# One token-gate phase ahead of the blocks: S5 and gate columns in seven block products over 1024 tokens, gates kept in DRAM

## The chip, the cores and the metric

The kernel runs on one core of one Trainium2 chip. The metric is the device time in microseconds (us) of one execution; of several runs the median counts. Engines are called PE (TensorE), DVE (VectorE), ACT (ScalarE), POOL (GpSimd) and SP (SyncE, which here only issues DMAs).

## The reference

The kernel is one gated layer over x (2048 tokens, 1024 columns, float32). Cut to what matters here:

```python
hn = rmsnorm(x, norm_w)
proj = hn @ w_in                     # 1024 x 10264 columns, split into the pieces below
ha = mlstm_chunkwise(aq, ak, av, i_pre, logf)       # branch a, recurrent in chunks
hb = gla_chunkwise(bq, bk, bv, log_a)               # branch b, recurrent in chunks
yc = gelu(s5_ssm(cu, ...))                          # branch c, 32 groups, scan over all 2048 tokens
yc = yc * sigmoid(yc @ s5_w_glu) * silu(cz)
ga, gb, gc = split(sigmoid(g), 3)                   # g: 3 x 1024 columns of proj
merged = ga * (ya @ w_a) + gb * (yb @ w_b) + gc * (yc @ w_c)
out = rmsnorm(x + merged @ w_out, final_norm)
```

The columns cu (512), cz (512) and g (3072) of proj need nothing but hn. The S5 scan needs cu of all tokens.

## The kernel before, in words

Every large product keeps float32 precision by splitting both operands into a rounded part "hi" and a rest "lo", and adding three matmuls: hi·hi, hi·lo, lo·hi. For a weight tile ACT makes hi by a copy (L85) and DVE makes lo by a subtraction (L86, function `split`); in some places POOL subtracts (L99, L105). A full product of 512 tokens by 512 columns over 1024 inputs is `dense_fm` (L110): 8 slices k, 4 column tiles, 3 terms, so 96 matmuls of 128x512 (L122 to L124).

Tokens go in four blocks b of 512. **Ahead of the blocks** stands a pre-phase over b = 3, 2, 1, 0: `norm(b)` (rmsnorm, transposes by PE at L192, split), `proj_c` (the columns u = cu and z = cz, each one `dense_fm`; the split u weights are kept for all four blocks), `spill(b)` (split hn of a block to DRAM, L197), and two pieces q of `s5_mats` (L930 on: the S5 matrices of four groups, eight pieces in all, made by DVE and POOL together at L948 to L977). `s5_setup` (L765 on) computes small S5 tables in some 200 DVE instructions.

**A block** then goes through `gla_in`, two `gla_pair`, `mlstm_gates` (its transposes at L513 mark a fixed place of each block), two `mlstm_pair`, and for the branches bi = 1, 0, 2: `gate(bi, f)` for two halves f (96 matmuls each, tanh by ACT at L654 into tiles `sg`), `branch` (`yl` tiles read back from DRAM at L664 to L669; matmuls with w_bb, w_ba, w_bc; DVE multiplies by the gate at L674, POOL adds at L679). `c_final` finishes S5's output for the block with a glu product, `start(b+1)` brings hn of the next block from DRAM and begins it, `tail` does w_out and the last norm. In block 0 the S5 scan itself, `s5_main` for 16 q's of two groups (L1005 to L1053), is put between the branches: matmuls zp (L1034), a copy by ACT, a swap of partition halves by two DMAs that ACT issues (L1025, L1026), a product by POOL (L1027), two DVE instructions (L1028, L1029), a DVE scan, a second such rotation, and matmuls yp (L1047, L1048).

A scheduler orders the instructions on each engine ahead of time; on the chip each engine runs its list in order, and SP and ACT issue their DMAs in order too.

Of the kernel before, what the change touches and what calls it, by code (L numbers as in the profile page):

```python
# [12 lines left out]
ALU = mybir.AluOpType  # L13
# [43 lines left out]
def hybrid_kernel(ctx: ExitStack, tc: tile.TileContext, a):  # L57
# [24 lines left out]
    z_d = dram.tile([NB, 4, 128, TB], F32, name="z_d")  # L82

# [6 lines left out]
    def wload(src, k, n, keep=None):  # L90
        if keep is not None and k in keep:
            return keep[k]
        raw = w_p.tile([128, 512], F32, tag="raw", name="raw", bufs=RB)
        nc.sync.dma_start(out=raw[:, 0:n], in_=src(k))
        if keep is not None:
            t = keep["pool"].tile([128, 2, 512], F32R, tag="keep", name="keep", bufs=KD)
            keep[k] = t[:, 0, :], t[:, 1, :]
            nc.scalar.copy(out=t[:, 0, :], in_=raw)
            nc.gpsimd.tensor_tensor(out=t[:, 1, :], in0=raw, in1=t[:, 0, :].bitcast(F32), op=ALU.subtract)  # L99
            return keep[k]  # L100
# [9 lines left out]
    def dense_fm(src, nk, n, tiles, rhs, evict, keep=None, cuts=1):  # L110
# [4 lines left out]
        for i in range(cuts):  # L115
            ts = slice(i * TB // cuts, (i + 1) * TB // cuts)
            for k in range(nk):
                hi, lo = wload(src, k, n, keep)
                rh, rl = rhs(k)
                for m, (o, mm) in enumerate(tiles):  # L120
                    pm = ps[m][0:mm, ts]
                    nc.tensor.matmul(pm, lhsT=hi[:, o:o + mm], rhs=rh[:, ts], start=(k == 0), stop=False)  # L122
                    nc.tensor.matmul(pm, lhsT=hi[:, o:o + mm], rhs=rl[:, ts], start=False, stop=False)  # L123
                    nc.tensor.matmul(pm, lhsT=lo[:, o:o + mm], rhs=rh[:, ts], start=False, stop=(k == nk - 1))  # L124
# [24 lines left out]

    def rsqrt(dst, src, n, pool, scale):  # L150
        v = pool.tile([128, 8], F32, tag="rsq", name="rsq", bufs=4)
        nc.vector.tensor_scalar(out=v[:, 0:n], in0=src, scalar1=scale, scalar2=EPS, op0=ALU.mult, op1=ALU.add)
        nc.gpsimd.tensor_tensor(out=dst, in0=v[:, 0:n], in1=mhalf[:, 0:n], op=ALU.pow)

    mat_d = dram.tile([32 // GB, 128, 3, GB, 128], F32, name="mat_d")
    cs_d = dram.tile([32 // GB, 128, GB, 2, NJ], F32, name="cs_d")
    rho = const.tile([128, 32], F32, name="rho")
    s5_cm = tc.tile_pool(name="s5", bufs=1, side="right")
    s5 = s5_cm.__enter__()
    hn = {}  # L160

    def hn_rhs(k):
        return hn[k // 4][:, k % 4, 0, :], hn[k // 4][:, k % 4, 1, :]

    with tc.tile_pool(name="pre", bufs=2) as pre:
        nwb = pre.tile([128, DM], F32, name="nwb", bufs=1)
        hns = {}
        keep = {"pool": pre}

        def norm(b):  # L170
            hb = []
            for g in range(2):
                t = (pre if b % 2 else hn_p).tile([128, 4, 2, TB], F32R, tag="hn", name="hn", bufs=2)
                hb.append(t)
            hns[b] = hb
            for c in range(NC):
                r0 = b * TB + c * CH
                xt = pre.tile([128, DM], F32, tag="xt", name="xt")
                nc.sync.dma_start(out=xt, in_=x[r0:r0 + CH, :])
                if b == NB - 1 and c == 0:  # L180
                    nc.sync.dma_start(out=nwb, in_=a["norm_w"].partition_broadcast(128))
                xn = pre.tile([128, DM], F32, tag="xn", name="xn")
                ss = pre.tile([128, 1], F32, tag="ss", name="ss")
                nc.scalar.activation(out=xn, in_=xt, func=AF.Square, accum_out=ss)
                rs = pre.tile([128, 1], F32, tag="rs", name="rs")
                rsqrt(rs, ss, 1, pre, 1.0 / DM)
                nc.vector.scalar_tensor_tensor(out=xn, in0=xt, scalar=rs, in1=nwb, op0=ALU.mult, op1=ALU.mult)
                for g in range(2):
                    pt = psm.tile([128, 4, 128], F32, tag="m", name="pt")
                    for i in range(4):  # L190
                        k = g * 4 + i
                        nc.tensor.transpose(pt[:, i, :], xn[:, k * 128:(k + 1) * 128], ident)  # L192
                    split(hb[g][:, :, 0, c * CH:(c + 1) * CH], hb[g][:, :, 1, c * CH:(c + 1) * CH], pt)

        def spill(b):
            for g in range(2):
                nc.sync.dma_start(out=hnd[b, :, 4 * g:4 * g + 4], in_=hns[b][g].bitcast(F32))  # L197

        def proj_c(b, part):
            hb = hns[b]  # L200

            def rhs(k):
                return hb[k // 4][:, k % 4, 0, :], hb[k // 4][:, k % 4, 1, :]

            def ev_u(m, ps):
                us = pre.tile([128, T8, JB], F32, tag="us", name="us")
                nc.scalar.copy(out=us, in_=ps.rearrange("p (j s) -> p s j", s=T8))
                nc.sync.dma_start(
                    out=u_d[:, 8 * m:8 * m + 8, :, b * JB:(b + 1) * JB].rearrange("s g h j -> (g h) s j"), in_=us)

            def ev_z(m, ps):
                th = pre.tile([128, TB], F32, tag="th", name="th")
                nc.scalar.activation(out=th, in_=ps, func=AF.Tanh, scale=0.5)
                zt = pre.tile([128, TB], F32, tag="zt", name="zt")
                nc.vector.scalar_tensor_tensor(out=zt, in0=th, scalar=1.0, in1=ps, op0=ALU.add, op1=ALU.mult)  # L215
                nc.sync.dma_start(out=z_d[b, m], in_=zt)

            if part == 0:
# [8 lines left out]
        for b in range(NB - 1, -1, -1):  # L227
            if b < NB - 1:
                proj_c(b, 0)
# [943 lines left out]
```

## Time and profile before

| quantity | value |
|---|---|
| median of 3 runs | 2986.44 us (2984.15 to 2987.95) |
| the profiled execution, its own time | 2983.99 us |
| its span in the trace | 2982.2 us |
| mean granted PE clock, share of full speed | 0.986 |
| busy: PE, PEld (weight load) | 96%, 82% |
| busy: DVE, ACT, POOL | 58%, 42%, 31% |
| DMA, mean over the span | 127 GB/s |

The span is what the trace covers; the execution's own time is 1.8 us longer. Matmuls are pipelined: each record lasts some 0.39 us while the next starts 0.23 us later, so the busy share of PE says little, and the count of matmuls in a stretch more. "PEclk" is the clock that was granted to PE, 1.00 being full speed.

### The profile page before, as it was taken

What the parts mean: (1) busy time and instruction counts of PE and PEld (TensorE: products, weight loads), DVE (VectorE), ACT (ScalarE), POOL (GpSimd) and SP (SyncE); (2) the same over time, 40 slices, a digit from 0 to 9 for tenths busy, and PEclk for the clock granted to TensorE, in tenths of its full rate; (3) what the DMA queues carried; (4) which work ended last, traced back from release to release, by engine and by line L of the source; (5) the groups of instructions that cost most, each with busy time, mean ns of one, the idle gap of its engine ahead of it and who ended that gap; (6) DMA issues with size and microseconds to landing.
All of it is one profiled execution on the core that took longest, in us unless ns stands there. A gap on an engine that the chain in (4) does not pass through costs nothing. (4 is left out here: it accounts for less than half of the span.)

```text
span 2982.2 us, 41294 instructions
## 1 busy us (share of the span) xinstructions
PE 2857.7 (96%) x14360; PEld 2446.0 (82%) x14360; DVE 1738.8 (58%) x3289; ACT 1257.8 (42%) x2512; POOL 912.1 (31%) x783
## 2 busy tenths in 40 slices
PE   7898899999889999999999999999999999999998
PEld 7677889887668798988888798988888798897886
DVE  8766675645465666665434558555434658656335
ACT  4324444432224544444333644444334544444333
POOL 3453453212330345231122245231122345321122
PEclk9999999999999999999999999999999999999999
DMA  7665223336866332334434332334445332334433
GB/s 246 227 207 168 63 75 103 103 104 165 227 194 215 106 109 75 92 85 118 143 117 157 121 103 64 98 89 122 137 117 169 112 95 69 98 94 145 144 114 103
DMA packets 291442, 379.74 MB, mean 127 GB/s; under 512 B 83936, under 2 KB 194960, under 8 KB 288928
## 3 DMA queue, kind: packets, MB, share of 16 engines
q1 hardware_dynamic: 286112, 368.70, 41.7%
q10 hardware_dynamic: 5120, 8.39, 1.1%
q8 instruction: 113, 1.85, 0.3%
q14 instruction: 97, 0.79, 0.1%
HBM read 302.33 MB, written 65.04 MB: 123 GB/s over the span
## 5 line engine op out<-in xcount | busy, mean ns | idle before, releaser
L86 DVE TENSOR_TENSOR wlo<-raw,whi 128x512 fp32r<-128x512 f32 (+2 forms) x736 | 551.8, 754 | 774.7 <-ACT whi L85 625.1
L85 ACT CAST whi<-raw 128x512 fp32r<-128x512 f32 (+2 forms) x736 | 421.0, 576 | 714.1 <-PE d L123 440.3
L122 PE MATMUL d<-hn,whi 128*128 128x512 f32 x1472 | 588.2, 400 | 13.8 <-ACT whi L85 12.5
L123 PE MATMUL d<-hn,whi 128*128 128x512 f32 x1472 | 581.2, 395 | 0.0
L124 PE MATMUL d<-hn,wlo 128*128 128x512 f32 x1472 | 552.4, 397 | 5.3 <-DVE wlo L86 4.9
L139 PE MATMUL d<-wlo,hn 128*128 128x384 f32 (+1 forms) x1280 | 440.7, 344 | 12.1 <-DVE wlo L86 9.9
L140 PE MATMUL d<-whi,hn 128*128 128x384 f32 (+1 forms) x1280 | 433.8, 339 | 0.0
L105 POOL TENSOR_TENSOR wlo<-raw,whi 128x384 fp32r<-128x384 f32 x208 | 237.3, 1141 | 529.4 <-ACT whi L104 348.4
L138 PE MATMUL d<-whi,hn 128*128 128x384 f32 (+1 forms) x1280 | 387.0, 347 | 2.6 <-DVE zt L215 1.6
L122 PEld LDWEIGHTS d<-hn,whi 128*128 128x128 f32 x1472 | 278.8, 189 | 78.0 <-ACT whi L85 16.0
L124 PEld LDWEIGHTS d<-hn,wlo 128*128 128x128 f32 x1472 | 277.5, 189 | 68.3 <-DVE wlo L86 7.7
L123 PEld LDWEIGHTS d<-hn,whi 128*128 128x128 f32 x1472 | 278.4, 189 | 57.2 <-issue 0.9
L139 PEld LDWEIGHTS d<-wlo,hn 128*128 128x128 f32 x1280 | 242.0, 189 | 19.3 <-DVE wlo L86 12.8
L138 PEld LDWEIGHTS d<-whi,hn 128*128 128x128 f32 x1280 | 236.0, 189 | 11.4 <-issue 2.9
L140 PEld LDWEIGHTS d<-whi,hn 128*128 128x128 f32 x1280 | 242.1, 189 | 0.5 <-issue 0.2
L669 POOL TENSOR_TENSOR yl<-yraw,yl 128x512 fp32r<-128x512 f32 x64 | 83.9, 1310 | 447.2 <-ACT yl L668 400.9
L122 PE MATMUL d<-yl,whi 128*128 128x512 f32 x512 | 204.6, 401 | 4.0 <-ACT whi L85 1.7
L123 PE MATMUL d<-yl,whi 128*128 128x512 f32 x512 | 202.6, 396 | 0.0
L104 ACT CAST whi<-raw 128x384 fp32r<-128x384 f32 x208 | 106.2, 510 | 201.8 <-PE d L140 141.2
L124 PE MATMUL d<-yl,wlo 128*128 128x512 f32 x512 | 188.6, 397 | 2.4 <-DVE wlo L86 2.4
L679 POOL TENSOR_TENSOR sg<-sg 128x512 f32<-128x512 f32 x64 | 92.8, 1477 | 108.4 <-DVE sg L674 108.4
L539 DVE SCALAR_TENSOR_TENSOR cacc<-craw,convw,cacc 128x512 f32<-128x512 f32 x144 | 121.7, 845 | 2.7
(334 smaller groups left out, 4647.9 us busy)
## 6 DMA issues: line engine op xcount, KB each, us to landing
raw<-in_w_in_dram SPq DMA_DIRECT2D x480, 192.0 KB
raw<-in_w_in_dram SPq DMA_DIRECT2D x232, 256.0 KB
yraw<-y_a SPq DMA_DIRECT2D x64, 256.0 KB
raw<-in_w_out_dram SPq DMA_DIRECT2D x64, 256.0 KB
hnd<-hn SPq DMA_DIRECT2D x6, 2048.0 KB
y_a<-ys SPq DMA_DIRECT2D x64, 192.0 KB
raw<-in_w_bb_dram SPq DMA_DIRECT2D x48, 256.0 KB
raw<-in_w_ba_dram SPq DMA_DIRECT2D x48, 256.0 KB
```

Of the source, the lines that this page charges most:

```text
L85: nc.scalar.copy(out=hi, in_=src)
L86: nc.vector.tensor_tensor(out=lo, in0=src, in1=hi.bitcast(F32), op=ALU.subtract)
L104: nc.scalar.copy(out=hi[:, 0:n], in_=raw[:, 0:n])
L105: nc.gpsimd.tensor_tensor(out=lo[:, 0:n], in0=raw[:, 0:n], in1=hi[:, 0:n].bitcast(F32), op=ALU.subtract)
L122: nc.tensor.matmul(pm, lhsT=hi[:, o:o + mm], rhs=rh[:, ts], start=(k == 0), stop=False)
L123: nc.tensor.matmul(pm, lhsT=hi[:, o:o + mm], rhs=rl[:, ts], start=False, stop=False)
L124: nc.tensor.matmul(pm, lhsT=lo[:, o:o + mm], rhs=rh[:, ts], start=False, stop=(k == nk - 1))
L138: nc.tensor.matmul(ps[c][:, 0:n], lhsT=lh[:, cs], rhs=hi[:, 0:n], start=(k == 0), stop=False)
L139: nc.tensor.matmul(ps[c][:, 0:n], lhsT=lh[:, cs], rhs=lo[:, 0:n], start=False, stop=False)
L140: nc.tensor.matmul(ps[c][:, 0:n], lhsT=ll[:, cs], rhs=hi[:, 0:n], start=False, stop=(k == nk - 1))
L539: nc.vector.scalar_tensor_tensor(out=acc, in0=raw[:, i:TB + i], scalar=convw[:, t, i:i + 1], in1=acc, op0=ALU.mult, op1=ALU.add)
L679: nc.gpsimd.tensor_tensor(out=acc[i], in0=acc[i], in1=sg[m], op=ALU.add)
```

## The change

A new function `early` takes the place of the pre-phase, and all work on the columns u, z and g moves there, for two blocks of tokens (a "pair": blocks 2 and 3 first, then 0 and 1) at a time.

One **quad** treats 256 columns by 1024 tokens over 1024 inputs. Weights and tokens are each cut into 2 by 2 halves; seven products of half size, with sums and differences of halves as operands, replace eight. A product is 4 slices by 3 terms, 12 matmuls of 128x512, so a quad has 84 matmuls. The token side (tiles T0 to T6, split into hi and lo) is built once per pair; the weight side per quad: POOL forms four sums or differences, ACT copies seven hi parts, DVE (5) and POOL (2) subtract for lo, and four evictions go through DVE, ACT and SP. Pair 1 has 14 quads (z0, z1, g0 to g11; u of these blocks is done by an ordinary product, `plain_u`), pair 0 has 16 (u, z, g).

In pair 1, after each of the quads j = 2 to 9, stands one piece of `s5_mats` and `ahead`, the norm of a quarter of block 0 or 1, put to DRAM. `second_load` and `second_pair` then build T0 to T6 of pair 0. In pair 0 the steps of `s5_main` are spread over quads 3 to 15. The tanh of the gates is stored in DRAM (`g_d`, 96 tiles of 256 KB) and `gate` in a block only loads it. In a block `c_final` now stands right behind `mlstm_pair`, the branches follow with no gate matmuls between them, and `start(b+1)` and `tail` close every block.

The core of the diff (after's lines; `...` marks what is left out):

```diff
-    def gate(bi, f):
+    def gate(b, bi, f):
         sg = []
-        def ev(m, ps):
+        for m in range(4):
             t = tl.tile([128, TB], F32, tag="t2", name="sg", bufs=T2B)
-            nc.scalar.activation(out=t, in_=ps, func=AF.Tanh, scale=0.5)
+            nc.sync.dma_start(out=t, in_=g_d[b, 8 * bi + 4 * f + m])
             sg.append(t)
-        dense_fm(win(GT + bi * DM + f * 512, 512), KD, 512, full(512), hn_rhs, ev)
         return sg
...
         acc = {}
-        for i, bi in enumerate((1, 0, 2)):
-            sg = [gate(bi, f) for f in range(2)]
...
+        c_final(nc, a, mx, tl, b, dskip, u_d, y_d, z_d, y_a, dense_fm, split, full)
+        for bi in (1, 0, 2):
+            sg = [gate(b, bi, f) for f in range(2)]
             yl = {}
             for f in range(2):
                 branch(b, acc, bi, f, sg[f], yl)
-                if b == 0 and i < 2:
-                    s5_steps(...)
-        if b and b + 1 < NB:
+        if b + 1 < NB:
             gi = start(b + 1)
         tail(b, acc)
...
+def early(tc, nc, a, hn_p, ident, rho, rsqrt, D):
+        def quad(c0, done):
+            raw = big("raw")...
+            nc.sync.dma_start(out=raw, in_=a["w_in"]...[:, :, c0:c0 + 256])
...
+            G.tensor_tensor(out=s1, in0=a21, in1=a22, op=A_)
+            G.tensor_tensor(out=s2, in0=s1, in1=a11, op=SB)
+            G.tensor_tensor(out=a21, in0=a11, in1=a21, op=SB)
...
+            product(pa, split(a11, V), 0, True, False)
+            ACT.copy(out=p1, in_=pa)
+            product(pb, split(s2, G), 1, True, False)
+            V.tensor_tensor(out=u2, in0=pb, in1=p1, op=A_)
+            G.tensor_tensor(out=s2, in0=a12, in1=s2, op=SB)
+            product(pa, split(a12, V), 2, False, True)
+            done(0, 0, pa, None)
+            product(pb, split(a21, V), 3, False, False)
+            V.tensor_tensor(out=u3, in0=pb, in1=p1, op=A_)
+            product(pc, split(s1, G), 4, True, False)
+            done(1, 1, pc, u3)
+            product(pb, split(a22, V), 5, False, True)
+            done(1, 0, pb, p1)
+            product(pc, split(s2, V), 6, False, True)
+            done(0, 1, pc, u2)
...
+        order = [("z", 0), ("z", 1)] + [("g", i) for i in range(12)]
...
+            for j, y in enumerate(order[:10]):
+                run(*y, 1)
+                if j >= 2:
+                    s5_mats(..., j - 2)
+                    ahead((j - 2) // 4, (j - 2) % 4)
...
+            F = second_load(hp)
+            for y in order[10:]:
+                run(*y, 1)
+            second_pair(F)
...
+            for j, y in enumerate([("u", 0), ("u", 1)] + order):
+                run(*y, 0)
+                to = max(0, min(n5, n5 * (j - 1) // 13))
+                for i in range(at, to):
+                    ... next(s5q[i - LAG[s]]) ...
```

In the whole program the matmuls of 128x512 for these columns go from 3072 (2304 for the gates, 768 for u and z) to 2712 (30 quads of 84, 192 for `plain_u`).

How the rows stand on three engines. **POOL in the stage of the S5 matrices.** In before one piece of `s5_mats` reads (m, P, W, fm are its tiles, `mk` a cleared one):

```order
L957 TENSOR_TENSOR m_1604<-raw_1598,pw 128x576
L959 TENSOR_TENSOR P_1613<-m_1604,m_1605 128x576
L957 TENSOR_TENSOR m_1604<-w_1606,pw 128x4x128
L959 TENSOR_TENSOR W_1617<-m_1604,m_1605 128x512
L975 TENSOR_TENSOR fm_1622<-low,high 128x512
L999 MEMSET mk 128x512
L975 TENSOR_TENSOR fm_1622<-low,high 128x512
L975 TENSOR_TENSOR fm_1632<-low,high 128x512 x2
```

In after the same piece (L1142 to L1184 now) stands between the quads' sums (s, raw; L857 to L859, L871) and lo parts (hl, L839):

```order
L857 TENSOR_TENSOR s_2210<-raw 128x512
L859 TENSOR_TENSOR raw<-raw 128x4x128
L1142 TENSOR_TENSOR m_2109<-raw_2103,pw 128x576
L858 TENSOR_TENSOR s_2211<-s_2210,raw 128x512
L1184 MEMSET mk 128x512
L1144 TENSOR_TENSOR P_2118<-m_2109,m_2110 128x576
L1142 TENSOR_TENSOR m_2109<-w_2111,pw 128x4x128
L1144 TENSOR_TENSOR W_2122<-m_2109,m_2110 128x512
L1160 TENSOR_TENSOR fm_2127<-low,high 128x512
L89 TENSOR_TENSOR rs<-rsq,mhalf 128x1
L1160 TENSOR_TENSOR fm_2127<-low,high 128x512
L839 TENSOR_TENSOR hl<-s_2211,hl 128x512
```

Two more fm, one hl and one s (L871) follow before the next quad: 14 large instructions per quad on POOL where the piece alone had eight.

**SP at the start.** In after the split hn of blocks 2 and 3 (hn, t_100 and T_91, 2 MB each) is written to DRAM ahead of loads of x (xt) and of the first quad's weights (raw, 1 MB):

```order
L738 DMA uraw<-in_w_in_dram 128x512 x3
L731 DMA hnd<-hn 128x4096 x2
L699 DMA xt<-in_x_dram 128x1024 x3
L754 DMA u_d<-us 128x8x64 x2
L738 DMA uraw<-in_w_in_dram 128x512
L699 DMA xt<-in_x_dram 128x1024
L754 DMA u_d<-us 128x8x64 x2
L738 DMA uraw<-in_w_in_dram 128x512 x7
L731 DMA hnd<-t_100 128x4096
L731 DMA hnd<-T_91 128x4096
L852 DMA raw<-in_w_in_dram 128x8x256
```

In before the same queue loads x and the first weights with no store between them; the loads of the first two token quarters and weights read:

```order
L179 DMA xt<-in_x_dram 128x1024
L181 DMA nwb<-in_norm_w_dram 128x1024
L179 DMA xt<-in_x_dram 128x1024
L94 DMA raw<-in_w_in_dram 128x512 x5
```

**ACT in the S5 scan.** In before the issues of the swaps stand almost alone among a few casts of weights (whi):

```order
L1035 COPY uz_6892<-zp 128x512
L1025 DMA ra_6899<-uz_6892 64x512
L1026 DMA ra_6899<-uz_6892 64x512
L1035 COPY uz_6918<-zp 128x512
L1025 DMA ra_6925<-uz_6918 64x512
L1026 DMA ra_6925<-uz_6918 64x512
L85 CAST whi<-raw 128x512 x2
L1025 DMA ra_6899<-ra_6899 64x512
```

In after one q is in the swaps at a time, and the quads' casts (hl) and tanh (sg) stand behind each issue:

```order
L1220 COPY uz_4926<-zp 128x512
L1210 DMA ra_4942<-uz_4926 64x512
L1211 DMA ra_4942<-uz_4926 64x512
L908 ACTIVATE sg<-pa 128x512
L838 CAST hl<-raw 128x512
L1210 DMA ra_4942<-ra_4942 64x512
L1211 DMA ra_4942<-ra_4942 64x512
L838 CAST hl<-s_4967 128x512
L838 CAST hl<-raw 128x512
L908 ACTIVATE sg<-sg 128x512
```

Between the first and the second issue of a q there are now one tanh and one cast.

## Rows read from the trace of the kernel before

**Rows 1.** The page's first part: the span, and the busy time of each engine.
```profile
span 2982.2 us, 41294 instructions
PE 2857.7 (96%) x14360; PEld 2446.0 (82%) x14360; DVE 1738.8 (58%) x3289; ACT 1257.8 (42%) x2512; POOL 912.1 (31%) x783
```

**Rows 2.** Four stretches: from:to, length; busy (records) per engine, PEclk, DMA share, GB/s.
```profile
0.00:75.00 75.00, 59.17 (x362) 53.10 (x363) 64.46 (x213) 35.85 (x67) 26.57 (x33) 1.00 0.78 246
75.00:150.00 75.00, 63.63 (x292) 51.02 (x290) 59.24 (x139) 22.90 (x41) 32.85 (x26) 0.91 0.69 229
700.00:905.00 205.00, 173.38 (x704) 134.27 (x703) 117.34 (x151) 52.51 (x93) 62.48 (x46) 0.97 0.73 200
2125.00:2225.00 100.00, 100.00 (x441) 82.33 (x440) 36.29 (x49) 30.56 (x52) 18.77 (x14) 1.00 0.39 113
```

**Rows 3.** Waits in the gate stage, 2125 to 2225: total us, times, longest.
```profile
ACT whi L85 <- PE d L123: 59.7, 26, 4.2
...
ACT yl L668 <- DMA yraw<-y_a: 10.3, 5, 3.6
```

**Rows 4.** PE by time (start us, us): first block product, then the L513 marks.
```profile
242.98 0.45 PE L138 MATMUL d<-whi,hn 128*128 128x408 f32 x1
...
499.52 0.60 PE L513 MATMUL ptg<-ident,gat 128*128 128x128 f32 x4
...
1251.24 0.60 PE L513 MATMUL ptg<-ident,gat 128*128 128x128 f32 x4
...
2561.04 0.60 PE L513 MATMUL ptg<-ident,gat 128*128 128x128 f32 x4
```

**Rows 5.** Single lines: times, duration ns (least, median, most), first and last start.
```profile
L86 DVE TENSOR_TENSOR wlo<-raw,whi x736: 525/685/3207, 27.2 to 2963.9; 128x512 fp32r<-128x512 f32 x108, 128x384 fp32r<-128x384 f32 x68, 128x408 fp32r<-128x408 f32 x8
...
L674 DVE SCALAR_TENSOR_TENSOR sg<-sg,d x96: 659/681/690, 691.0 to 2928.0; 128x512 f32<-128x512 f32 x96
...
L669 POOL TENSOR_TENSOR yl<-yraw,yl x64: 1267/1293/1807, 655.9 to 2905.6; 128x512 fp32r<-128x512 f32 x64
```

**Rows 6.** DVE by time, one piece of s5_mats (103.18 to 123.83).
```profile
103.18 0.23 DVE L948 TENSOR_TENSOR m<-raw,s5c 128x64 f32<-128x64 f32 x1
103.32 0.22 DVE L949 TENSOR_TENSOR m<-raw,s5c 128x64 f32<-128x64 f32 x1
...
105.65 1.67 DVE L86 TENSOR_TENSOR wlo<-raw,whi 128x512 fp32r<-128x512 f32 x1
...
120.85 0.68 DVE L86 TENSOR_TENSOR wlo<-raw,whi 128x512 fp32r<-128x512 f32 x1
121.45 1.55 DVE L976 TENSOR_TENSOR fm<-low,high 128x512 f32<-128x512 f32 x1
123.83 0.22 DVE L948 TENSOR_TENSOR m<-raw,s5c 128x64 f32<-128x64 f32 x1
```

**Rows 7.** POOL by time in the same piece.
```profile
105.08 1.68 POOL L957 TENSOR_TENSOR m<-raw,pw 128x576 f32<-128x576 f32 x1 [2.66 <-DVE w L950]
...
121.02 1.44 POOL L975 TENSOR_TENSOR fm<-low,high 128x512 f32<-128x512 f32 x1 [2.26 <-DVE CS L977]
```

**Rows 8.** PE by time: the first transposes of the program.
```profile
8.65 1.97 PE L192 MATMUL pt<-ident,xn 128*128 128x128 f32 x8 [8.65 <-DVE xn L187]
```

**Rows 9.** The S5 scan: PE by time (x2: two passes of one product).
```profile
726.34 0.59 PE L1048 MATMUL yp<-uz,mt 128*128 128x255 f32 x2
726.77 0.59 PE L1047 MATMUL yp<-uz,mt 128*128 128x256 f32 x2
...
736.81 0.67 PE L1034 MATMUL zp<-uz,mt 128*128 128x256 f32 x2 [2.93 <-ACT whi L85]
...
738.55 1.06 PE L1048 MATMUL yp<-uz,mt 128*128 128x255 f32 x2
```

**Rows 10.** The S5 scan: ACT's first and second swap issue of one q, by time.
```profile
701.69 0.52 ACTq L1025 DMA_DIRECT2D ra<-uz  x1
...
713.38 0.47 ACTq L1025 DMA_DIRECT2D ra<-ra  x1
```

More of the change, by code (lines that the diff above doesn't have):

```diff
@@ L88, in hybrid_kernel, with wload @@
     pool_lo = [False]
-    def wload(src, k, n, keep=None):
-        if keep is not None and k in keep:
-            return keep[k]
+    def wload(src, k, n):
         raw = w_p.tile([128, 512], F32, tag="raw", name="raw", bufs=RB)
         nc.sync.dma_start(out=raw[:, 0:n], in_=src(k))
[L95 to L100, printed above, removed]
         hi = w_p.tile([128, 512], F32R, tag="whi", name="whi", bufs=WB)
@@ L108, in wload, with dense_fm @@
         return hi, lo
-    def dense_fm(src, nk, n, tiles, rhs, evict, keep=None, cuts=1):
+    def dense_fm(src, nk, n, tiles, rhs, evict):
         ps = []
@@ L114, in dense_fm @@
             ps.append(p)
[L115 to L124, printed above, removed]
+        for k in range(nk):
+            hi, lo = wload(src, k, n)
+            rh, rl = rhs(k)
+            for m, (o, mm) in enumerate(tiles):
+                pm = ps[m][0:mm, :]
+                nc.tensor.matmul(pm, lhsT=hi[:, o:o + mm], rhs=rh, start=(k == 0), stop=False)
+                nc.tensor.matmul(pm, lhsT=hi[:, o:o + mm], rhs=rl, start=False, stop=False)
+                nc.tensor.matmul(pm, lhsT=lo[:, o:o + mm], rhs=rh, start=False, stop=(k == nk - 1))
         for m in range(len(tiles)):
@@ L148, in full @@
         return [(i * 128, 128) for i in range(n // 128)]
[L150 to L218, printed above, removed]
-                dense_fm(win(CU, 512), KD, 512, full(512), rhs, ev_u, keep, 2 if b == NB - 1 else 1)
-            else:
-                dense_fm(win(CZ, 512), KD, 512, full(512), rhs, ev_z)
-        norm(NB - 1)
-        proj_c(NB - 1, 0)
-        sgn = ld("sgn", [128, 1])
-        s5t = s5_setup(nc, a, s5, rho, sgn)
-        for b in range(NB - 1, -1, -1):
-            if b < NB - 1:
-                proj_c(b, 0)
-            if b:
-                norm(b - 1)
-            proj_c(b, 1)
-            if b:
-                spill(b)
-            for q in ((3 - b) * 2, (3 - b) * 2 + 1):
-                s5_mats(nc, a, s5, s5t, psm, ident, mat_d, cs_d, q)
-        hn.update(enumerate(hns[0]))
@@ L717, in tail @@
                      m_lhs, ev_o)
-    nq = 32 // GM
-    s5q = [s5_main(nc, a, mx, s5t, psm, mat_d, cs_d, u_d, y_d, q) for q in range(nq)]
-    def s5_steps(i0, i1):
-        for i in range(i0, i1):
-            for st in (2, 1, 0):
-                if 0 <= i - LAG[st] < nq:
-                    next(s5q[i - LAG[st]])
     def start(b):
@@ L748, in hybrid_kernel @@
         acc = {}
-        for i, bi in enumerate((1, 0, 2)):
-            sg = [gate(bi, f) for f in range(2)]
-            if i == (0 if b else 2):
-                c_final(nc, a, mx, tl, b, dskip, u_d, y_d, z_d, y_a, dense_fm, split, full)
-            if b == 0 and i == 2:
-                gi = start(1)
+        c_final(nc, a, mx, tl, b, dskip, u_d, y_d, z_d, y_a, dense_fm, split, full)
+        for bi in (1, 0, 2):
+            sg = [gate(b, bi, f) for f in range(2)]
             yl = {}
@@ L766, in s5_setup @@
+def s5_setup(nc, a, s5, rho):
+    sgn = s5.tile([128, 1], F32, name="sgn")
+    nc.sync.dma_start(out=sgn, in_=a["sgn"])
     lre = s5.tile([128, 32], F32, name="lre")
@@ L1035, in s5_main @@
     nc.scalar.copy(out=zs, in_=zp)
[L1036 removed]
+    ra = mx.tile([128, 2, GM * NJ], F32, tag="ra5", name="ra5", bufs=1)
     sw, sc = half(ra, 0), half(ra, 1)
```

251 lines of the change are left out of this document (236 added, 15 removed).

## The prediction

> **What bounds the kernel now.** I read the page's first part first: PE is busy for 96% of the span, DVE for 58%, POOL for 31% [rows 1]. The matmul count by stretch says where that busy share is real. In the gate stage PE starts 441 matmuls in 100 us, so one of 128x512 costs 100 / 441 = 0.227 us, at full clock [rows 2]. There ACT waits for PE (59.7 us) and not PE for ACT [rows 3]: that stage is bound by PE, and every matmul taken out of it is worth its 0.227 us. Other stretches differ. From 75 to 150 us PE starts 292 in 75 us, many of them short, at a granted clock of 0.91; the S5 scan, 700 to 905, holds 704 records [rows 2], of which 192 are passes of S5's own products (16 q of 6 products, two passes each) at half of 726.77 - 726.34 = 0.43 us [rows 9]. 512 x 0.227 + 192 x 0.215 = 157.5 us of PE work in 205: 47.5 us are lost there. So this kernel has stages where PE sets the time and stages where DVE, POOL and transfers do, and the change moves PE work from the first kind into the second.
>
> In the S5-matrix stage it is DVE and POOL that matter, and they stand in each other's way. A DVE subtraction from two SBUF tiles has a median of 0.685 us but reaches 3.2 us; one with a PSUM operand (L674) never leaves 0.66 to 0.69 [rows 5]. By time, the same subtraction takes 0.68 us at 120.85 and 1.67 us at 105.65, while POOL's 1.68 us instruction runs; the one at 121.45 takes 1.55 beside POOL's 1.44 us instruction [rows 6, 7]. So I count the two engines' SBUF-reading work as one queue: DVE 0.60 us an instruction (121.45 - 120.85), POOL 1.27 (its least) [rows 5, 6].
>
> **What is saved.** PE issues 3072 - 2712 = 360 fewer matmuls of 128x512: 82 us by 0.227. If all else were covered, the profiled 2984 us would become 2902. The rest asks what of it is given back.
>
> **The early phase, in order of time.**
>
> *Start to the second quad.* Shared DVE and POOL work: `plain_u` splits 16 weights, 8 on each engine, 8 x 0.60 + 8 x 1.27 = 15 us; the split of block 2, 8 on POOL, 10; block 3's sums and splits, per quarter 6 on DVE and 4 on POOL, 4 x 8.7 = 35; `s5_setup`, 209 small DVE instructions at 103.32 - 103.18 = 0.14 us [rows 6], 29; two quads at 6 x 1.27 + 5 x 0.60 = 10.6 us, 21. Sum 110. Ahead of it lie the 8.65 us to the first transposes [rows 8]. The four spills of 2 MB now go ahead of x and of the first quad's weights on SP: 8.4 MB at the 246 GB/s of the start [rows 2] are 34 us. Sum 153; PE's own work there (192 + 168 matmuls, 82 us, and transposes) lies beside it. Ends: 115 if the spills overlap wholly, 175 if the first products also wait for the sums one after another. I take **153**.
>
> *Eight quads with a piece of s5_mats each.* In before a piece takes 123.83 - 103.18 = 20.65 us [rows 6] with six weight subtractions of 0.60 in it, so 17.0 by itself; a quad's 10.6 us come on top: 27.6, and the norm's small POOL instruction, **28 us**. PE's work in such a quad is 84 x 0.227 = 19.1 and about 2 for transposes and small products, 21.3. So DVE and POOL bind, 8 x 28 = **224**. Ends: 21.3 each (170 in all) if the quads' instructions fill gaps of the piece, 33 (264) if POOL's order holds the next quad's sums behind a piece that waits. The Trainium skill, page SBUF — State Buffer, section Who interferes with whom, has one exclusive lock for the ports that DVE's second SBUF input and GpSimd share. By that rule a quad with a piece is the sum of both engines' instructions, 14 x 1.27 + 15 x 0.60 + 6 x 0.14 = 27.6 us, so the sum of the stage would be 221; stretches in rows 6 and 7 agree with it, the ports themselves no row shows.
>
> *Four plain quads:* 76. POOL 7.6 and DVE 3.0 fit twice beneath 19.1 us.
>
> *Second pair.* T0 to T6 have one buffer each, so the last products of pair 1 free them one by one while about 35 us of DVE and POOL work (14 halves of puts, sums, four splits, each twice as long as an instruction above) refill them; PE can start as T0 is there but then catches up. Ends 8 (only T0 exposed) and 22; I take **15**.
>
> *Sixteen quads:* 16 x 19.07 = **305**; S5's own products 192 x 0.215 = **41**. S5's losses: 47.5 us in before; the 19 steps now spread over 13 quads (some 290 us in place of 205), so more matmuls lie between steps, while the round from the first to the second swap issue, 713.38 - 701.69 = 11.7 us [rows 10], stands in ACT's order ahead of casts that the quads need. I take 0.7 of 47.5, **33**; ends 10 and 70. For the way out of the phase and for clock drops (after PE stood for 2.93 us at 736.81 the two passes at 738.55 take 1.06 in place of 0.59 us, the lower of the two levels, 1.2 GHz [rows 9]) 6 + 5 = **11**.
>
> Early phase: 153 + 224 + 76 + 15 + 305 + 41 + 33 + 11 = **858 us**.
>
> **The blocks.** The first block product starts at 242.98, the marks stand at 499.52, 1251.24, 2561.04 [rows 4]. Without its 576 gate matmuls (576 x 0.227 = 130.8 us) a block takes (2561.04 - 1251.24) / 2 - 130.8 = 524.1. Start to first mark 256.5, three block steps 1572.3, last mark to the end 2982.2 - 2561.04 - 130.8 = 290.4: **2119 us**. That assumes that nothing loses the cover of the gate matmuls. It does lose some: the chains of the last chunks of `mlstm_pair`, `c_final`'s DVE work, and the 4 MB of hn and 24 gate tiles per block on SP now have 524 us in which PE has fewer independent matmuls. The write of y and its reading back is such a wait; reading cost ACT 10.3 us in five waits even under the gates [rows 3]. I take 7.5 us a block, **30**; ends 0 and 100 (a whole 25 us per block, 17 of it the transfer of 4 MB at 246 GB/s). The 96 tanh move with their matmuls; their 25 MB of stores and 25 MB of loads (96 tiles of 256 KB each way) add some 17 GB/s to a mean of 127, far from the 246 of the start [rows 2].
>
> **Sum.** 858 + 2119 + 30 = 3007 us of span, with 1.8 us around it 3009: 25 us above the profiled execution (2984) and 23 above the median (2986.44). Of the 82 us saved, the S5-matrix quads give back 54, the start, second pair and blocks more.
>
> **Rivals.**
>
> *The queue does not bind (faster).* If DVE and POOL interleave as well in the quads as PE needs, the eight quads fall to 170 and the blocks lose nothing: 858 - 54 + 2119 + 2 = 2925. For it: in before the DVE and POOL had gaps in a piece (POOL 2.66 and 2.26 us of idle in rows 7). Against: the piece's chain alternates between them. It decides if a piece's quad takes under 25 us.
>
> *The clock falls (slower still).* In the eight quads PE would idle a quarter of the time. In before, the stretch with most idle had 0.91 granted [rows 2] and passes at half speed [rows 9]. At 1.2 GHz the quad's PE part is 2 x 21.3 = 43 us, above 28; the clock decides as its mean in these quads falls under 21.3 / 28 = 0.76, and at the low level for half of them adds about 70: 3080. The Trainium skill, page TensorE: Matmul & The Clock Gate, section HAM oscillation — how this bites in real kernels, has idle gaps between groups of matmuls throttle PE again each time; by that rule these eight quads would run at the low level, no long stretch here does.
>
> *The blocks lose their cover* at the upper end: 100 in place of 30, 3079.
>
> *The S5 scan binds the second pair's quads:* ACT behind the second swap issue, 5 us more for each of 13 quads: 3074.
>
> *The saving isn't there:* the counts of matmuls come from the instruction lists, so this has no chance of its own.
>
> **How the numbers follow.** A measurement of this kernel can tell about 0.2%, 6 us, from no change: 2980 to 2992 is "same". Forecast 0.48, with its own range 2970 to 3050 (0.07 faster, 0.08 same, 0.33 slower); the queue does not bind 0.25 (faster); clock 0.12, blocks 0.10, S5 scan 0.05 (slower). Faster 0.32, same 0.08, slower 0.60. The range takes half of the first rival, 2925, and reaches the clock's 3080 with a little over it: 2925 to 3085.
>
> **What the profile after would show.** Right: 28 us from quad to quad in the eight quads, DVE subtractions of over 1.2 us there, POOL near always busy, PE with idle time put down to hi or lo parts; 19.1 us in the plain quads; the first block product near 858; marks 524 to 532 apart. Wrong: quads of 21 us with a piece in them, or marks over 545 apart, or a granted clock under 0.76 in the eight quads.

## The result, and the profile after

The changed kernel takes 3051.73 us (median of 3, 3050.29 to 3056.79) against 2986.44 us: **slower**, ratio 1.0224 with a 95% interval of 1.02 to 1.0247. The forecast was 3009 us, slower by 23; it became slower by 65. The profiled execution is the longest of the three, 3056.79 us, with a span of 3054.7, so spans are compared with the 3007 us of the sum.

The page's first part for after answers to [rows 1]:

```profile
span 3054.7 us, 40831 instructions
PE 2840.3 (93%) x13905; PEld 2392.6 (78%) x13905; DVE 1940.5 (64%) x3399; ACT 1295.8 (42%) x2556; POOL 1255.4 (41%) x1004
```

PE has fewer instructions and the kernel is longer: PE stands more often, and POOL is busy 343 us longer than in [rows 1]. The table of stretches shows where (from:to, length; then busy time and records of PE, PEld, DVE, ACT and POOL; granted PE clock; DMA share; GB/s):

```profile
50.00:75.00 25.00, 7.93 (x41) 6.25 (x39) 20.61 (x24) 21.19 (x34) 19.57 (x15) 0.67 0.54 150
...
157.00:383.00 226.00, 191.67 (x815) 147.29 (x814) 189.49 (x304) 79.42 (x138) 163.84 (x121) 0.92 0.55 178
383.00:465.00 82.00, 80.28 (x347) 63.88 (x345) 48.38 (x48) 38.18 (x62) 57.08 (x34) 1.00 0.50 171
465.00:502.00 37.00, 24.37 (x84) 17.84 (x85) 29.84 (x17) 13.55 (x19) 35.74 (x18) 0.82 0.72 240
502.00:880.00 378.00, 344.62 (x1453) 273.97 (x1451) 220.46 (x258) 115.74 (x207) 169.25 (x124) 0.98 0.53 159
...
1774.00:1824.00 50.00, 42.07 (x205) 33.74 (x204) 29.44 (x71) 23.80 (x50) 9.49 (x9) 0.93 0.61 188
```

From 50 to 75 us PE has 8 of 25 us of work while DVE and POOL build the sums of the first pair, and its clock is 0.67. 157 to 383 are the eight quads with a piece of `s5_mats`, 28.3 us each; 383 to 465 four plain quads; 465 to 502 the first quad of the second pair, in which PE is busy for 24 of 37 us and POOL for 35.7; the last stretch lies in a block, below. PE's own row of time gives the borders: the first quad with a piece begins here, the first plain quad and the second pair here, then the first block product, then the fixed mark of each block (the L513 of [rows 4], now L433; start us, us). Where the text gives quads, a quad is 84 of the 2520 product matmuls in the order of their starts:

```profile
157.13 0.40 PE L847 MATMUL pb<-T,hl 128*128 128x512 f32 x1
...
383.37 0.40 PE L846 MATMUL pa<-hn,hl 128*128 128x512 f32 x1
...
465.03 0.51 PE L846 MATMUL pa<-hn,hl 128*128 128x512 f32 x1 [0.78 <-ACT hl L838]
...
880.55 0.71 PE L151 MATMUL d<-whi,hn 128*128 128x408 f32 x1 [9.39 <-ACT whi L108]
...
1134.05 0.49 PE L433 MATMUL ptg<-ident,gat 128*128 128x128 f32 x3
...
1674.04 0.49 PE L433 MATMUL ptg<-ident,gat 128*128 128x128 f32 x3
...
2213.18 0.60 PE L433 MATMUL ptg<-ident,gat 128*128 128x128 f32 x4
...
2752.92 0.49 PE L433 MATMUL ptg<-ident,gat 128*128 128x128 f32 x3
```

Set beside the sum:

| part | forecast, us | measured, us |
|---|---|---|
| start to the first quad with a piece | 153 | 157 |
| eight quads with a piece | 224 | 226 |
| four plain quads | 76 | 82 |
| second pair to the first block product | 405 | 415.5 |
| first block product to first mark | 256.5 | 253.5 |
| three steps from mark to mark | 3 x 531.6 | 3 x 539.6 |
| last mark to the end | 297.9 | 301.8 |

(7.5 us of lost cover are in each of the last two lines' forecast.) The early phase is 22.5 us longer than forecast, the blocks 25.

**What PE waits for in a block.** The largest stop stands in the same place of blocks 0 to 2, about 128 us behind the mark (in the last block no stop there is over 1.1 us); PE by time:

```profile
1801.99 0.33 PE L541 MATMUL sb<-v,mkt 128*64 128x193 f32 x1
1801.99 0.33 PE L542 MATMUL sb<-v,mkt 128*64 128x193 f32 x1
1808.69 2.08 PE L135 MATMUL d<-yr,whi 128*128 128x512 f32 x4 [6.37 <-ACT yr L108]
1810.57 0.63 PE L136 MATMUL d<-yr,whi 128*128 128x512 f32 x1
1810.99 0.63 PE L137 MATMUL d<-yr,wlo 128*128 128x512 f32 x1
...
1813.06 0.40 PE L136 MATMUL d<-yr,whi 128*128 128x512 f32 x1
1813.30 0.40 PE L137 MATMUL d<-yr,wlo 128*128 128x512 f32 x1
```

The chunk of `mlstm_pair` is issued, and the next matmul in PE's list is the glu product of `c_final`, whose operand yr is still being made (loads of y and u, DVE and ACT in turn). PE stands for 6.4 us, and then for some 4 us its matmuls take 0.63 in place of 0.40 us and start 0.42 us apart in place of 0.24: the granted clock is 0.50 from 1808.69 to 1813, the lower of the two levels (1.2 GHz). By my estimate that costs some 2 us, so the stop and the clock behind it cost about 8. Before the change gate matmuls stood there, which waited for nothing but a weight.

### The profile page after: what moved, and what is told of

Same layout as the page of the kernel before. It is cut to its first block, busy times and chain, and to the rows that moved or that the text cites. A ratio compares the mean times of both kernels' runs of the same rounds, so it can differ in the third digit from the quotient of the medians.

```text
span 3054.7 us, 40831 instructions
## 1 busy us (share of the span) xinstructions
PE 2840.3 (93%) x13905; PEld 2392.6 (78%) x13905; DVE 1940.5 (64%) x3399; ACT 1295.8 (42%) x2556; POOL 1255.4 (41%) x1004
## 5 line engine op out<-in xcount | busy, mean ns | idle before, releaser
L109 DVE TENSOR_TENSOR wlo<-raw,whi 128x384 fp32r<-128x384 f32 (+2 forms) x512 | 394.1, 774 | 509.8 <-ACT whi L108 477.2
L108 ACT CAST whi<-raw 128x384 fp32r<-128x384 f32 (+2 forms) x512 | 283.5, 557 | 435.0 <-PE d L136 207.2
L152 PEld LDWEIGHTS d<-wlo,hn 128*128 128x128 f32 x1280 | 242.8, 190 | 15.5 <-DVE wlo L109 9.0
L151 PEld LDWEIGHTS d<-whi,hn 128*128 128x128 f32 x1280 | 236.6, 189 | 17.1 <-ACT whi L108 9.8
L135 PE MATMUL d<-hn,whi 128*128 128x512 f32 x576 | 233.6, 405 | 8.3 <-ACT whi L108 8.3
L136 PE MATMUL d<-hn,whi 128*128 128x512 f32 x576 | 229.2, 398 | 0.0
L137 PE MATMUL d<-hn,wlo 128*128 128x512 f32 x576 | 210.4, 401 | 3.4 <-DVE wlo L109 2.9
L846 PE MATMUL pb<-T,hl 128*128 128x512 f32 x360 | 151.0, 419 | 21.9 <-DVE u L876 12.0
L839 DVE TENSOR_TENSOR hl<-raw,hl 128x512 fp32r<-128x512 f32 x120 | 128.9, 1076 | 43.9 <-ACT hl L838 40.2
L848 PE MATMUL pb<-T,hl 128*128 128x512 f32 x360 | 147.7, 410 | 5.0 <-POOL hl L839 5.0
L847 PE MATMUL pb<-T,hl 128*128 128x512 f32 x360 | 147.1, 409 | 0.0
L135 PEld LDWEIGHTS d<-hn,whi 128*128 128x128 f32 x576 | 108.7, 189 | 35.3 <-ACT whi L108 10.0
```

Of the source, the lines that this page charges most:

```text
L108: nc.scalar.copy(out=hi, in_=src)
L109: nc.vector.tensor_tensor(out=lo, in0=src, in1=hi.bitcast(F32), op=ALU.subtract)
L135: nc.tensor.matmul(pm, lhsT=hi[:, o:o + mm], rhs=rh, start=(k == 0), stop=False)
L136: nc.tensor.matmul(pm, lhsT=hi[:, o:o + mm], rhs=rl, start=False, stop=False)
L137: nc.tensor.matmul(pm, lhsT=lo[:, o:o + mm], rhs=rh, start=False, stop=(k == nk - 1))
L151: nc.tensor.matmul(ps[c][:, 0:n], lhsT=lh[:, cs], rhs=hi[:, 0:n], start=(k == 0), stop=False)
```

## The experiments

All times beside their own runs of the kernel before on the same chip (medians 2981.68 to 2988.82).

**POOL's piece work without reads** (after with, in `s5_mats`):

```diff
-        G.tensor_tensor(out=m0[:, :, 0:n], in0=x..., in1=pr, op=M)
+        for _ in range(2):
+            G.memset(m0[:, :, 0:n], 0.0)
...
-        G.tensor_tensor(out=out, in0=m0[:, :, 0:n], in1=m1[:, :, 0:n], op=A_)
+        for _ in range(2):
+            G.memset(out, 0.0)
...
-            G.tensor_tensor(out=f0, in0=x, in1=hr, op=M)
+            for _ in range(2):
+                G.memset(f0, 0.0)
```

> Left out: in the pieces of s5_mats every POOL product or sum is replaced by two POOL memsets of the same tile (about 1.05 us for 1.27), so the S5 matrices are not computed; POOL stays nearly as long in the piece, but its piece work reads nothing. Theory A (DVE's two-input work and POOL's reads go one after another): DVE subtractions in the eight quads fall from over 1 us to about 0.7, a quad with a piece falls from 28.3 to PE's 21 to 23 us, quad 2 to quad 10 from 226 to 170 to 185 us, the kernel 40 to 55 us under after. Rival B (lists in order: POOL's sums behind a piece's waits, ACT behind late loads of x): only the 8 x 0.2 us per piece shorter POOL work shows, 24 to 27 us a quad, 10 to 30 us under after.

There is one run of it: 3027.21 us against 2981.68, span 3025.4, so 24.5 us under after. The stretch of the eight quads fell to 197 us (24.6 a quad). Both numbers lie in the range of rival B; the DVE subtractions fell as theory A had it. Groups by line in 157 to 383 (busy us, mean ns | idle before), first after, then this run:

```profile
L839 DVE TENSOR_TENSOR hl<-raw,hl 128x512 fp32r<-128x512 f32 x31 | 34.4, 1109 | 0.0
L1162 DVE TENSOR_TENSOR CS<-fm,fm 128x512 f32<-128x512 f32 x31 | 32.6, 1050 | 3.6 <-POOL fm L1160 2.9
L1161 DVE TENSOR_TENSOR fm<-low,high 128x512 f32<-128x512 f32 x31 | 32.1, 1036 | 4.4 <-POOL W L1144 4.1
...
L888 DVE TENSOR_TENSOR sg<-pc,u 128x512 f32<-128x512 f32 x15 | 10.2, 679 | 0.0
```

```profile
L1165 DVE TENSOR_TENSOR CS<-fm,fm 128x512 f32<-128x512 f32 x32 | 25.3, 792 | 15.3 <-POOL fm L1163 13.6 <-DMA cs_d<-CS 1.7
L1164 DVE TENSOR_TENSOR fm<-low,high 128x512 f32<-128x512 f32 x32 | 23.5, 735 | 0.4
...
L1163 POOL MEMSET fm<- 128x512 f32 x62 | 33.0, 533 | 18.8 <-DVE CS L1165 15.4 <-DVE rsq L88 1.8
```

The same DVE instructions go from 1.04 and 1.05 us to 0.735 and 0.79 when POOL writes at its side but reads nothing; the eviction sg, which has a PSUM operand, takes 0.68 us in after as well. So DVE's two-input work and POOL's reads do hold each other up. The stage lost 29 of the 56 us that the eight quads take above PE's 170, but how much of that is due to the reads is not shown, since the edit takes away more: a memset waits for no operand, so the tile W is ready early as well, and two memsets are shorter than one product. In after PE waits 25.2 us for W (the lines stand under the run with a buffer for x); in this run that wait is gone. PE stands still for 226 - 191.67 = 34.3 us of the stage in after, for 17.1 here, and its clock is higher:

```profile
158.00:355.00 197.00, 179.91 (x813) 140.37 (x812) 162.16 (x297) 78.08 (x136) 136.01 (x174) 0.98 0.62 200
```

**Sums of weight halves on DVE in the eight quads** (`run(*y, 1, V if j >= 2 else G)`, and in `quad`, S being the engine handed in):

```diff
-            G.tensor_tensor(out=s1, in0=a21, in1=a22, op=A_)
+            S.tensor_tensor(out=s1, in0=a21, in1=a22, op=A_)
```

and so for the other three sums.

> In quads j = 2 to 9 the four sums of weight halves go from POOL to DVE. Theory A (POOL's reads and DVE's two-input work one after another, some 1.1 us for a POOL instruction and 0.60 for one of DVE): 4 x 0.5 = 2 us less per quad, quad 2 to quad 10 at 207 to 214 us in place of 226, 12 to 20 us under after. Rival B (each engine has its own limit, and DVE with 19 large instructions and its evictions has the longer list): no gain, or up to 10 us slower.

The eight quads take 367.3 - 155.9 = 211.4 us, in the range that theory A gave, with 19 large DVE instructions per quad. But the kernel measured 3051.64 us, ratio 1.0226 (1.021 to 1.0241): the same as after. Quads 10 and 11 behind the stage now take 22.5 and 27.3 us in place of 20.5 and 19.6; the first block product starts 8 us earlier, at 872.7. In this trace the blocks then take 8 us more, though their code is the same as in after; over the traces with that code they vary by 10 us (2172.6 in the run with pieces spread, 2182.6 here), so a gain of 8 us can be lost in that.

**A buffer of its own for x:**

```diff
-            xt = hl((128, DM), F32, "xt")
+            xt = xp[0].tile([128, DM], F32, tag="xt", name="xt", bufs=1)
```

> The tile xt that takes x from DRAM has a buffer of its own in place of one of the five that all hi and lo tiles share, so that loads of x need not wait for a quad's tiles. Theory C (the late loads of x, 15.5 us of ACT's waits at the start and 54.9 us in the eight quads, hold the casts behind them on ACT): the first quad starts 5 to 12 us earlier, a quad with a piece takes 25 to 27 us, 15 to 30 us under after in all. Theory A alone (the shared DVE and POOL time binds there): ACT's waits go, the quads stay at 27.5 to 28.5, and the kernel gains under 10 us, at the start only.

In after the waits in 157 to 383 begin with (line waited for: us in total, times, longest):

```profile
ACT xn L708 <- DMA xt<-in_x_dram: 54.9, 6, 10.8
PEld pt L1171 <- POOL W L1144: 27.8, 6, 5.4
PE pt L1171 <- POOL W L1144: 25.2, 6, 4.9
```

The first of them is gone in this run, and its eight quads take 377.7 - 165.9 = 211.8 us, as theory C said (26.5 a quad). The start, though, came out 8.8 us later (165.9 in place of 157.1), and the quad behind the stage takes 26.3 us: 3060.3 us, ratio 1.0251 (1.0236 to 1.0266), nothing won. Quad 11 starts at 404.0 as in after (403.8): what the stage won, the start and the next quad lost, so it is not shown that x's late loads cost anything by themselves. The third row is a wait that I had not counted, PE's list holding the transposes of W until POOL is done: six stops, 25.2 of the 34.3 us for which PE stands still. In the traces of the four runs that shorten the stage (POOL without reads, sums on DVE, a buffer for x, and below all two-input work on DVE) these stops are gone, but for one of 2.68 us and some of under 0.8; PE stands still for 17 to 27 us there, in other stops. No run takes the wait for W away alone.

**Pieces spread over ten quads:**

```diff
-            for j, y in enumerate(order[:10]):
+            at = (2, 3, 4, 6, 7, 8, 10, 11)
+            for j, y in enumerate(order[:12]):
                 run(*y, 1)
-                if j >= 2:
+                if j in at:
```

> The eight pieces go over ten quads (j = 2, 3, 4, 6, 7, 8, 10, 11) in place of eight in a row. Theory A (shared DVE and POOL time): the ten quads need 8 x 17.0 + 10 x 10.6 = 242 us of it in place of the 226 + 40 = 266 that quads 2 to 11 take now, so 15 to 25 us under after. Rival B (a piece costs PE some 8 us wherever it stands, by waits in the lists): quads with a piece stay at 28, those without at 20, no change beyond 5 us; later loads for the second pair may add up to 10 us in both cases.

Rival B's total was right: quad 2 to quad 12 takes 419.8 - 157.7 = 262 us, against 423.4 - 157.1 = 266 in after. Quads with a piece take 22.1 to 30.2 us (27 on the mean), the two without 22.6 and 22.1. 3062.51 us, ratio 1.0269 (1.0252 to 1.0286). So most of the spare DVE and POOL time in a quad without a piece is of no use to the others. That this is because a piece's work stands in the lists within its own quad is argued, not shown.

**Spills later** (three of four `spill` calls moved to quad 2):

```diff
-                spill(2, g, T[2 * g])
-                spill(3, g, (t12, T[6])[g])
+            spill(3, 0, t12)
...
+                if j == 2:
+                    spill(2, 0, T[0])
+                    spill(2, 1, T[2])
+                    spill(3, 1, T[6])
```

> Three of the four 2 MB spills (T0, T2, T6) are moved to quad 2. Theory: in after ACT waits 15.5 us for x in the start and POOL 15.1 us in one piece behind it, since the spills stand ahead of x on SP; without them the first quad starts 12 to 18 us earlier (84 to 90 in place of 102), and the kernel is 8 to 18 us under after. Rival: DVE and POOL work (110 us to quad 2) binds the start and not the loads; the first quad starts under 5 us earlier and the kernel within 5 us of after.

3059.63 us, ratio 1.0257 (1.0237 to 1.0276), the first quad at 103.7. This decides nothing: the scheduler put the spills where they had been (SP issues them at 29.56 and 80.14 in this run, at 29.56 and 79.08 in after). What spills elsewhere would bring was not tried in another way.

**c_final behind the first branch:**

```diff
-        c_final(nc, a, mx, ...)
         for bi in (1, 0, 2):
...
                 branch(b, acc, bi, f, sg[f], yl)
+            if bi == 1:
+                c_final(nc, a, mx, ...)
```

> c_final stands behind the first branch (w_bb) in every block, no longer right behind mlstm_pair. Theory: the stop of PE in the first chunk of the second mlstm pair (6.4 us for yr of c_final, then a slow clock, some 12 us lost per block) comes from the glu product standing there with operands that are still being made; with w_bb's 144 matmuls first it is covered: marks 530 instead of 539.6 us apart, 35 to 50 us under after. Rival: the chunk chain of mlstm_pair itself is what PE waits for and any product there only fills in part; marks 537 to 540 apart, within 12 us of after.

The marks stand 538.7 to 539.9 us apart, 3061.27 us, ratio 1.0262 (1.0245 to 1.028): the rival's number. But the stop of the theory is gone from its place, and another one of the same length has come, further on in the block. PE by time:

```profile
1861.63 0.55 PE L224 MATMUL pty<-ident,y 128*128 128x128 f32 x3 [0.68 <-POOL y L566]
1868.47 2.08 PE L135 MATMUL d<-yl,whi 128*128 128x512 f32 x4 [6.29 <-ACT yl L585]
```

ACT beside it:

```profile
1867.80 0.62 ACT L585 CAST yl<-yraw 128x512 fp32r<-128x512 f32 x1 [4.70 <-DMA yraw<-y_a]
```

w_b's and the glu's matmuls had been used up beside the chunks, and w_a's first operand is the last y of `mlstm_pair`, which goes to DRAM and back.

**c_final before the second mlstm_pair, branches in the order b, c, a:**

```diff
+        c_final(nc, a, mx, ...)
         mlstm_pair(b, 1, tg)
-        c_final(nc, a, mx, ...)
-        for bi in (1, 0, 2):
+        for bi in (1, 2, 0):
```

> In every block c_final is called ahead of the second mlstm_pair, and the branches come in the order b, c, a (1, 2, 0), so that the glu product's operands are long made when PE comes to it, and w_b's and w_c's matmuls stand between the last chunk of mlstm_pair and w_a, which must wait for y through DRAM. Theory A (the 15 us that a block loses against its matmul count are one uncovered wait of some 6 us, for yr in after and for y in the run with c_final behind the first branch, and the slow clock behind it): marks 526 to 530 us apart in place of 539.6, 35 to 50 us under after. Rival B (the chunks themselves need the time, whatever stands beside them): marks 536 to 540.

Worse: 3075.54 us, ratio 1.0298 (1.0281 to 1.0316), marks 542.6 to 551.6 apart. The stop for yr moved forward with `c_final`:

```profile
1704.73 2.08 PE L135 MATMUL d<-yr,whi 128*128 128x512 f32 x4 [5.75 <-ACT yr L108]
```

Three orders, three places, 5.75 to 6.4 us each time, for yr or for y. Whatever is put first is the product that waits; what is missing is work without a wait.

**One half of branch b's gates in the blocks again** (quads g4 and g5 dropped in both pairs):

```diff
+            if (bi, f) in [(1, 0)]:
+                def ev(m, ps): ... activation(..., func=AF.Tanh, scale=0.5) ...
+                dense_fm(win(GT + bi * DM + f * 512, 512), KD, 512, full(512), hn_rhs, ev)
+                return sg
...
+        sg = [gate(b, 1, f) for f in range(2)]
         c_final(nc, a, mx, ...)
```

> One half of one branch's gates (branch b, f = 0: 512 columns) is computed in the blocks again, by 96 matmuls from hn as in before, right behind mlstm_pair; its four quads (g4 and g5 of both pairs) are left out of the early phase. PE then does 4 x 96 - 4 x 84 = 48 matmuls more (11 us). Theory A (a block loses some 13 us because at the end of mlstm_pair PE has nothing to do that is ready, and its clock falls): the stop goes, a block's step is 539.6 + 21.8 - 10 to 13 = 548 to 551 us, the early phase is 75 to 100 us shorter, the kernel 25 to 45 us under after. Rival B (the stop is the chunks' own, or moves to the next product): a block's step is 558 to 562, the kernel within 10 us of after.

The marks are 549.9 to 552.9 us apart, at the upper end of theory A's 548 to 551, for 96 matmuls more (21.8 us) per block than after's 539.6. Ten us a block come back, and the stop of 6.4 us is gone from all blocks. Stretches of 50 us around the end of `mlstm_pair`, this run:

```profile
1727.00:1777.00 50.00, 50.00 (x251) 41.90 (x250) 32.52 (x73) 25.92 (x52) 7.19 (x8) 1.00 0.66 193
1747.00:1797.00 50.00, 50.00 (x235) 39.22 (x234) 35.69 (x79) 25.61 (x50) 7.73 (x7) 1.00 0.89 293
```

PE is busy throughout at full clock, as the kernel before was in the same place (1351 to 1401: 50.00 of 50, 1.00), where after has 42.07 at 0.93. The kernel gained less than theory A's 25 to 45 us: 3046.08 us, 5.7 under after, which is rival B's number, ratio 1.0198 (1.0182 to 1.0213). With two plain quads fewer in each pair the load and building of the second pair is no longer covered (the quad at the border takes 49.7 us in place of 37.0, PE waiting 23.8 us of it for one cast), and the S5 steps stand in fewer quads, which then take up to 32 us.

With both halves in the blocks:

> Both halves of branch b's gates are computed in the blocks, eight quads are left out of the early phase. Theory A: the second half has no stop left to cover, so it costs its 48 matmuls more (11 us) and no more, less what quads with S5 steps lose now: within 15 us of the run with one half; marks 570 to 574 us apart. Rival: one half did not cover all, and the second brings another 15 to 30 us.

The marks are 570.2 to 573.0 us apart, 20 to 21 more than with one half: the second half covers nothing further. The kernel, at 3096.55 us, ratio 1.037 (1.0352 to 1.0388), is far worse, since two quads at the pairs' border now take 57 and 51 us. My bound of 15 us had left the early phase out.

**The three gains together** (half a gate product, sums on DVE, own buffer for x):

> One half of branch b's gates in the blocks, the four sums of the quads with a piece on DVE, and an own buffer for x in that stage. If the three gains are of different stages and add up: the run with one half of the gates less 10 to 25 us, about 2990 to 3010 us. If sums on DVE and the buffer for x shorten the same wait, only 5 to 10 us under the run with one half.

3055.54 us, ratio 1.023 (1.0213 to 1.0247): they do not add up; the kernel is 9 us slower than with the half gate product alone, outside both expectations. The eight quads end at 356.9 in place of 383.4, but the next three take 27.9, 42.3 and 50.2 us.

**All two-input work of the start, the first ten quads and the second pair on DVE:**

```diff
-                put(T[2 * g], c, s, G)
+                put(T[2 * g], c, s, V)
...
-                G.tensor_tensor(out=q1, in0=f3[0], ...)
+                V.tensor_tensor(out=q1, in0=f3[0], ...)
...
-            sub(G, t1, f12, f11)
+            sub(V, t1, f12, f11)
```

and so for the other instructions of that kind.

> All two-input work of the start, of the first ten quads and of the second pair's building goes from POOL to DVE; only the pieces' own products stay on POOL. Theory A (one queue of DVE 0.60 and POOL some 1.1 us an instruction wherever they are dense): start to quad 2 at 138 to 150 us in place of 157, quad 2 to quad 10 at 195 to 212 in place of 226, the pause between the pairs (465 to 502) 8 to 14 us shorter, the kernel 25 to 50 us under after. Rival (DVE's own list becomes the limit, with ten evictions and norms besides): the stages gain under 5 us each, the kernel stays within 12 us of after.

Each of the three stages came out as theory A had it: quad 2 at 142.1 (157.1), quad 2 to quad 10 in 205.9 us (226.3), the first quad of the second pair in 24.9 us (37.0). That is 47 us won, but the blocks start only 17.5 us earlier, at 863.06 in place of 880.55: the four plain quads behind the stage take 97.4 us in place of 81.7, and the quads with S5 steps, whose code is the same, 14 us more. 3041.61 us, ratio 1.0175 (1.016 to 1.0191), 10 us under after: the stages of theory A, the kernel of the rival.

With half a gate product in the blocks:

> The same, and one half of branch b's gates in the blocks. If the gains add up: 10 us less per block against its matmuls and the early gain, 2995 to 3020 us, at best near the kernel before (2986). If not: 3035 to 3050, as with the half gate alone.

3035.12 us, ratio 1.0152 (1.0135 to 1.017): the gains do not add up here either. It is the fastest of the versions that compute everything, and still 46 us slower than before. No version tried beats the kernel before.

## Why the prediction was wrong

The direction held, the size did not: 65 us slower where 23 were forecast. The measured 3051.73 us lies within the outer range, 2925 to 3085, and 2 us above the forecast's own, 2970 to 3050. Of the mechanisms, the blocks' was right and priced too low, the eight quads' was right in part.

*The step that failed* is the term for the blocks' lost cover: "I take 7.5 us a block, 30; ends 0 and 100". Measured, a step is 539.6 us against 524.1 by the count of matmuls, so 15.5 us a block. I had listed the waits (`mlstm_pair`'s last chunks, `c_final`, y through DRAM), but no row of the trace before gave the 7.5 us. The runs showed that in each order of the three products that was tried one of these waits stands open in blocks 0 to 2, 5.75 to 6.4 us long, and that the clock then falls for what follows, which I had counted for the early phase only: about 8 us together. Half a gate product brought ten of the 15.5 us back; where the other five go stays open. Of the 48 us by which the sum fell short, this term is 25 (the first part of the blocks came out 3 us shorter); some 5 of the 48 us come from the profiled execution being the longest of three.

*The early phase* came out 22.5 us too long, in four small pieces: start 4, eight quads 2, plain quads 6, second pair and S5 steps 10.5. No run shows that the spills cost the 34 us that the start's sum gives them; POOL's work there on DVE brought 15 us. A plain quad's 10.6 us of DVE and POOL work fit once beneath its 19.1, not twice as I wrote. At the pairs' border 37.0 us go for 19.1 of matmuls, 18 lost where I took 15; POOL is busy for 35.7 of them, and DVE in its place brought 12 us back. By my own prices the work there is 49 us, not about 35 (POOL 13 instructions of double length and four single ones, DVE nine double).

*The eight quads*: 224 forecast, 226 measured, and that it came so near is partly luck. Of the signs that I named only the 28 us came: DVE's subtractions of weights took 1.11 us on the mean and not over 1.2, POOL was busy for 163.84 of 226 us and not near always, and PE's idle time went for the most part to W and not to hi or lo parts. With POOL's reads gone, and the wait for W with them, 29 us went, not 54. I had taken the dense piece of [rows 6] as DVE and POOL time alone, while waits between the two engines were in its 20.65 us as well [rows 7]. How the 56 us divide among the shared time, PE's list waiting for W, the clock behind such stops and late loads of x is not shown. The spread run fits this: a total of DVE and POOL time is a bound for a stage only as far as the lists let work move from quad to quad.

*PE's saving* was real: in the first three plain quads 84 matmuls take 20.5, 19.6 and 19.6 us, where 96 at 0.227 would take 21.8.

*The rivals.* The first was to hold if a piece's quad took under 25 us; the eight quads took 28.3. The clock fell in them to 0.92 on the mean (the row 157 to 383; before had 0.91 from 75 to 150 [rows 2]), not under the 0.76 from which it would have decided. With two levels that is some 36 of the 226 us at the lower one, an estimate, so the clock has a part in the 28 us all the same. (Half of the quads at the low level would have added 4 x (43 - 28) = 60 us, not about 70.) The Trainium skill, page TensorE: Matmul & The Clock Gate, section HAM oscillation — how this bites in real kernels, tells of a kernel that is throttled again at each wait between its groups of matmuls; this trace agrees only in part, the quads were at the low level for a short time each and not throughout. After the single stop of 6.4 us matmuls did run at 0.63 us in place of 0.40. The blocks' loss, 55 us in place of 30, went a third of the way from there to its upper end of 100. The S5 scan took about what I gave it: the second and third quad of the second pair, which have no steps, take 21.3 and 21.8 us, those with steps 23 to 30.

## What to carry to other kernels

Before work that waits for nothing is moved out of a stage, look at what it stands beside: here 576 gate matmuls per block were also the cover for waits of some 6 us, one of which always came to the front, and leaving 96 of them behind returned ten of the 15 us lost. Price a stage that DVE and POOL share by the sum of DVE's two-input instructions and POOL's reading ones, and prefer DVE for such work there (0.60 us for some 1.1, by the pair of 1.68 us below); but read a dense stretch for its waits too before calling it full. A gain in one stage of lists that run in order is only kept if the next stage can start earlier: sums on DVE won 15 us in their stage and nothing that the kernel's time shows.

## What the runs showed that was not expected

In one stretch of after where both engines have work without a pause, 59.66 to 65, their starts alternate: DVE's lines by time, then POOL's:

```profile
60.17 1.75 DVE L728 TENSOR_TENSOR t<-F,t 128x512 fp32r<-128x512 f32 x1
61.84 1.75 DVE L781 TENSOR_TENSOR F<-f,F 128x512 f32<-128x512 f32 x1
63.52 1.75 DVE L728 TENSOR_TENSOR T<-F,T 128x512 fp32r<-128x512 f32 x1
65.20 0.68 DVE L779 TENSOR_TENSOR F<-F 128x512 f32<-128x512 f32 x1
65.80 0.68 DVE L728 TENSOR_TENSOR T<-F,T 128x512 fp32r<-128x512 f32 x1
```

```profile
59.66 1.71 POOL L780 TENSOR_TENSOR F<-F 128x512 f32<-128x512 f32 x1
61.34 3.39 POOL L728 TENSOR_TENSOR T<-F,T 128x512 fp32r<-128x512 f32 x2
```

Each instruction starts 1.67 or 1.68 us behind the last one on its engine, so a pair of one DVE and one POOL instruction costs 1.68 us, a little under the 0.60 + 1.27 = 1.87 that I added up. As POOL pauses, DVE's instructions start 0.60 us apart again. The Trainium skill, page SBUF — State Buffer, section Who interferes with whom, says that a GpSimd instruction which only writes does not contend with DVE's second input; the memset run agrees (0.735 us in place of 1.036 for the same DVE instruction).
